# A hybrid decoder step: first rows scaled in pieces, and loads, stores and a product given other places

## Chip, cores and metric

The kernel runs on one core of one Trainium2 chip. The core has TensorE (PE in the profile) for matrix products and transposes, VectorE (DVE), ScalarE (ACT), GpSimd (POOL) and SyncE (SP), which issues most of the transfers between HBM and the on-chip memory; a transfer's work is done by 16 DMA engines. Each engine runs its own instructions in order, and semaphores make one wait for another. The metric is the device time of one execution in microseconds, as a median over runs.

## What is computed

One layer for a prompt of 2048 tokens behind 16 learned "meta" tokens, and one new token for each of 8 sequences that have a cache. The width is 1024. Eight attention heads of 64 use stick-breaking weights; four groups of 128 channels are averaged over trailing windows of 2, 4, 8 and 16 tokens. Cut to what matters:

```python
h = rmsnorm(xp, norm_mix_g)              # xp: 16 meta rows, then the prompt
q, k, v, u = project_mix(h, w_in)        # 1024 -> 4 x 512
z = q @ k^T * ATTN_SCALE + sb_bias       # per head, key before query
a = exp(log_sigmoid(z) + suffix sums of -softplus(z) over later keys)
o_pool = (window mean of u - u) @ pool_w * pool_scale    # per group
xp = xp + concat([a @ v, o_pool]) @ w_out
xp = xp + conv_ffn(rmsnorm(xp, norm_ffn_g))  # 1024 -> 2 x 2816, width-3 conv, silu gate, -> 1024
y = rmsnorm(xp, norm_final_g)
```

rmsnorm multiplies a row by 1/sqrt(mean of squares + 1e-6) and by a gain. The same runs for the eight new tokens against their cached keys and values.

## The kernel before

**Tiles and products.** The prompt is cut into four chunks of 512 tokens, the width into eight blocks of 128. The normalised input is kept transposed, a tile `hk` per block and chunk (128 features x 512 tokens), split into a high and a low part in a shorter float format (fp32r). A product in full precision is three matmuls (`mm3`, lines 164 to 168): high by high, high by low, low by high. Weights come as raw 128x1024 tiles `wr` and are split into `wh` (a cast on ACT, line 160) and `wl` (a subtraction on DVE, line 161).

**The start.** `prep_first` (line 236) loads the first four tiles of 128 rows, squares them on ACT with a sum per row (`squares`), makes 1/rms of all four at once (`rstd_from`, an integer guess and three Newton steps on DVE), scales each 128x1024 tile on DVE (`times_r`), and then calls `turned` for each block: four transposes on PE (line 222, tile `tpx`), the gain and the high part on ACT (line 225), the low part on DVE (226), and a spill of the pair to HBM, `hs_s`, by SP (228), from which later head pairs load it again. `prep_small` does the same for 24 rows (8 new tokens, 16 meta rows), kept as `hsml`.

**Projection and attention.** The work is cut by g into four groups: two heads and 128 pooled channels each. For each g, chunk and kind (q, k, v, u: `step(g, ch, ki)`) a projection of 24 matmuls writes a 128x512 tile `kf`, which goes to HBM as q_s, k_s or rows of the outputs. At the first chunk `load_w` brings the weights in pairs (q, k and then v, u), and `few_rows` runs the 24 rows through each pair, 32 small matmuls (line 302), a transpose (`tq`, line 307) and stores, of which the meta rows of keys, queries and values are needed by attention. While chunk ch is projected, `prep_squares` and `prep_piece` prepare chunk ch+1 (tiles `xp` of 256 columns). Behind (1, 3), `fold_pool` multiplies the group's pooling weights by four rows' blocks of w_out, so that pooling and output projection become one (`pkf`, `pkw`, lines 393 to 405).

Attention works on units of 128 queries by up to 512 keys, 45 for each pair of heads. `fetch` loads keys (line 469), values (487) and queries: a group of 256 queries of one head is a tile `qr`, whose 64 feature rows are loaded twice, into the upper and the lower half of the 128 partitions (lines 457 and 458), since the keys' high and low parts lie stacked there; the tile is split into `qh` and `ql`. The first group of a pair has the 16 meta queries alone. `chain` computes the scores `z` for each of the two heads (line 518), both sigmoids on ACT (`om`, `be`), the running product by a scan on DVE (529), and multiplies `be` by the shifted scan (534), for one head on GpSimd and for the other on DVE. `turn` transposes the result (`tt`, line 572) and `weigh` multiplies it by the values.

**What sets the order.** The list `fill` holds the projection steps and preparations in program order, with `with_params` (the conv parameters, turned by PE at lines 636 and 637, and sums of the pooling state) as second entry; the loop behind it calls as many fill steps ahead of each unit as its keys need. The compiler's scheduler then fixes each engine's instruction order by a timeline of its own. SP's queue holds the loads and stores of all these parts in one order.

Behind the attention come the output projection, the ConvFFN in two halves (tiles `psu` and `psd`, the larger part of the span) and the eight new tokens, which the change doesn't touch but for `rstd_from`.

Of the kernel before, what the change touches and what calls it, by code (L numbers as in the profile page):

```python
# [19 lines left out]
P = 128  # L20
# [41 lines left out]
def hymba_kernel(  # L62
# [74 lines left out]
    def rstd_from(pool, ss, n):  # L137

        w = ss.shape[1]
        ms = pool.tile([P, w], F32, name=f"ms{w}")  # L140
        nc.vector.tensor_scalar(out=ms[:n, :], in0=ss[:n, :], scalar1=1.0 / D, scalar2=EPS, op0=ALU.mult, op1=ALU.add)
# [3 lines left out]
        nc.vector.tensor_single_scalar(ti[:n, :], ms[:n, :].bitcast(I32), 1, op=ALU.logical_shift_right)  # L145
        nc.vector.tensor_scalar(out=ri[:n, :], in0=ti[:n, :], scalar1=-1.0, scalar2=float(0x5F3759DF),
                                op0=ALU.mult, op1=ALU.add)
        for _ in range(3):
            if w == 1:
                nc.vector.scalar_tensor_tensor(out=t[:n, :], in0=r[:n, :], scalar=r[:n, 0:1], in1=ms[:n, :],  # L150
                                               op0=ALU.mult, op1=ALU.mult)
            else:
                nc.vector.tensor_tensor(out=t[:n, :], in0=r[:n, :], in1=r[:n, :], op=ALU.mult)
                nc.vector.tensor_tensor(out=t[:n, :], in0=t[:n, :], in1=ms[:n, :], op=ALU.mult)
            nc.vector.tensor_scalar(out=t[:n, :], in0=t[:n, :], scalar1=-0.5, scalar2=1.5, op0=ALU.mult, op1=ALU.add)
            nc.vector.tensor_tensor(out=r[:n, :], in0=r[:n, :], in1=t[:n, :], op=ALU.mult)
# [44 lines left out]

    def load_x(i, tag, bufs):
# [15 lines left out]
    def turned(ch, c, part):  # L218
# [9 lines left out]
        nc.sync.dma_start(out=hs_s[ch][c], in_=f32(hk))  # L228
# [7 lines left out]
    def prep_first():  # L236
        ss = pb.tile([P, 4], F32, name="ss4")
        xts = [load_x(1 + a, "be", BEB) for a in range(4)]
        gains()
# [3 lines left out]
        for a in range(4):  # L243
            times_r(xts[a], r[:, a:a + 1])
        hks[0] = []
        for c in range(NK):
            turned(0, c, lambda a: xts[a][:, c * P:(c + 1) * P])
# [39 lines left out]
    def load_w(g, kind):  # L287
        ft = 4 * "qkvu".index(kind) + g
        wr = pa.tile([P, NK, P], F32, name="wr", bufs=2)
        nc.sync.dma_start(out=wr, in_=w_in[:, ft * P:(ft + 1) * P].rearrange("(c p) f -> p c f", p=P))  # L290
        wh = pa.tile([P, NK, P], F32R, name="wh", bufs=4)
        wl = pa.tile([P, NK, P], F32R, name="wl", bufs=4)
        split(wh, wl, wr)
        return wh, wl, wr

    def few_rows(g, pair, w):
# [3 lines left out]
        for c in range(NK):  # L300
            for j in range(2):
                nc.tensor.matmul(ps[32 * j:32 * j + 32, :], hsml[:, c, :], w[pair[j]][2][:, c, :],
# [45 lines left out]
    tails = {}  # L348
# [40 lines left out]

    def fold_pool(g):  # L390
# [862 lines left out]
```

## Time and profile before

| | us |
|---|---|
| three runs | 2767.65, 2768.55, 2773.09 |
| their median | 2768.55 |
| the profiled execution, its own time | 2771.54 |
| its span, first to last instruction | 2769.8 |
| ACT busy in the span | 1031.4 |

The profile is of one execution, 3.0 us above the median of the runs. Busy times don't count instructions that only issue transfers. Its 40 slices show where PE rests and at which granted clock (tenths; 9 is 90% or more):

```profile
PE   5899999999998999999999999999999999999998
PEclk9899999999999999999999999999999999999999
DMA  7653552454425433455556555646656574666551
```

A slice is 69 us: the first holds the start with half of PE's time unused, the second the first units of attention. The groups of costly instructions are nearly all the ConvFFN's products, at some 0.39 us each, which follow each other closely; the start of the program is therefore read from windows and waits, not from the groups.

### The profile page before, as it was taken

How to read it: one execution, taken by the hardware profiler on the slowest of the kernel's cores; microseconds unless marked ns; L12 is line 12 of the kernel's file. 1: busy time of each engine (PE TensorE's matmuls, PEld its weight loads, DVE VectorE, ACT ScalarE, POOL GpSimd, SP SyncE). 2: the span in 40 equal slices, each digit the busy share in tenths (PEclk: the TensorE clock that was granted, in tenths of full speed). 3: DMA queues.
4: the chain of work that ended last, by engine and by line, in shares of the span. 5: the costliest groups of instructions: out<-in, count | busy, mean ns of one | idle time of the engine just before them, and what ended most of it. 6: DMA issues, size and time to landing. Idle time of an engine off the chain costs nothing.

```text
span 2769.8 us, 39760 instructions
## 1 busy us (share of the span) xinstructions
PE 2662.7 (96%) x14759; PEld 2089.6 (75%) x14759; DVE 1805.2 (65%) x3037; ACT 1031.4 (37%) x1833; POOL 721.7 (26%) x736
## 2 busy tenths in 40 slices
PE   5899999999998999999999999999999999999998
PEld 4677777787786888778877777777776777777776
DVE  4588768857669588669977777777774541114434
ACT  4466656655557256423322222222222320012111
POOL 0012212211122011145554554445554200000000
PEclk9899999999999999999999999999999999999999
DMA  7653552454425433455556555646656574666551
GB/s 252 218 178 118 167 179 97 130 203 136 165 87 171 159 117 101 147 193 193 184 208 242 207 201 213 227 165 237 215 206 237 173 258 165 200 205 212 179 194 64
DMA packets 326375, 498.79 MB, mean 180 GB/s; under 512 B 25367, under 2 KB 238631, under 8 KB 309781
## 3 DMA queue, kind: packets, MB, share of 16 engines
q1 hardware_dynamic: 307749, 362.03, 39.8%
q0 software_dynamic: 18432, 134.23, 12.7%
q8 instruction: 116, 1.90, 0.3%
q14 instruction: 78, 0.64, 0.1%
HBM read 395.99 MB, written 100.59 MB: 179 GB/s over the span
## 4 chain that ended last, share of the span: by engine, by line
PE 79%; DVE 3%; issue 2%; DMA 2%; ACT 1%; POOL 0%; SPq 0%; DVEq 0%; ACTq 0%; POOLq 0%
PE psu L166 12%; PE psu L167 12%; PE psu L168 12%; PE psd L166 6%; PE psd L168 6%; PE psd L167 6%; PE po L615 4%; PE z L518 3%; PE tt L572 3%; PE dav L950 2%; PE psm L166 2%; PE psm L168 2%; PE psm L167 2%; PE pso L167 2%; PE pso L166 2%; PE pso L168 2%
## 5 line engine op out<-in xcount | busy, mean ns | idle before, releaser
L166 PE MATMUL psu<-h2c,uwh 128*128 128x512 f32 x1408 | 555.0, 394 | 4.0 <-ACT uwh L160 2.2
L168 PE MATMUL psu<-h2c,uwl 128*128 128x512 f32 x1408 | 550.7, 391 | 1.3 <-DVE uwl L161 1.3
L167 PE MATMUL psu<-h2c,uwh 128*128 128x512 f32 x1408 | 551.6, 392 | 0.0
L534 POOL TENSOR_TENSOR be<-be,om 128x512 f32<-128x512 f32 (+3 forms) x176 | 182.6, 1037 | 844.2 <-DVE om L529 302.0
L1048 DVE SCALAR_TENSOR_TENSOR cv<-psu,par,cv 128x511 f32<-128x511 f32 x352 | 261.2, 742 | 146.5 <-ACT cv L1045 142.9
L166 PEld LDWEIGHTS psu<-h2c,uwh 128*128 128x128 f32 x1408 | 265.2, 188 | 81.1 <-issue 10.9
L1059 POOL TENSOR_TENSOR cv<-cv,cv 128x512 f32<-128x512 f32 x88 | 224.7, 2554 | 388.6 <-DVE cv L1053 290.7
L168 PEld LDWEIGHTS psu<-h2c,uwl 128*128 128x128 f32 x1408 | 265.3, 188 | 63.7 <-issue 7.3
L167 PEld LDWEIGHTS psu<-h2c,uwh 128*128 128x128 f32 x1408 | 265.3, 188 | 62.1 <-issue 8.5
L529 DVE TENSOR_TENSOR_SCAN om<-om,zero 128x513 f32<-128x513 f32 (+1 forms) x224 | 274.0, 1227 | 46.2 <-ACT om L519 41.2
L519 ACT ACTIVATE om<-z,nbias 128x512 f32<-128x512 f32 (+5 forms) x360 | 213.3, 593 | 138.3 <-PE z L518 83.4
L1045 ACT ACTIVATE cv<-psu,par 128x512 f32<-128x512 f32 x176 | 136.4, 776 | 289.1 <-PE psu L168 289.1
L1220 DVE TENSOR_TENSOR xt<-psd,xt 128x512 f32<-128x512 f32 x64 | 44.0, 691 | 281.8 <-PE psd L168 281.7
L520 ACT ACTIVATE be<-z,bias 128x512 f32<-128x512 f32 (+5 forms) x360 | 211.4, 589 | 0.6 <-PE tt L572 0.6
L167 PE MATMUL psm<-hk,wh 128*128 128x512 f32 x512 | 206.6, 404 | 2.9 <-DVE hk L226 2.9
L166 PE MATMUL psm<-hk,wh 128*128 128x512 f32 x512 | 205.0, 406 | 1.9 <-ACT hk L225 1.3
L168 PE MATMUL psm<-hk,wl 128*128 128x512 f32 x512 | 204.2, 399 | 1.0 <-DVE wl L161 1.0
L161 DVE TENSOR_TENSOR uwl<-uwr,uwh 128x1024 fp32r<-128x1024 f32 x94 | 121.1, 1290 | 127.8 <-ACT uwh L160 127.8
L166 PE MATMUL psd<-wd,ah 128*128 128x512 f32 x512 | 200.3, 395 | 0.0
L167 PE MATMUL psd<-wd,ah 128*128 128x512 f32 x512 | 200.0, 392 | 0.0
L168 PE MATMUL psd<-wd,al 128*128 128x512 f32 x512 | 199.4, 390 | 0.0
L160 ACT CAST uwh<-uwr 128x1024 fp32r<-128x1024 f32 x94 | 98.8, 1054 | 246.4 <-PE psu L167 230.4
(245 smaller groups left out, 4773.8 us busy)
## 6 DMA issues: line engine op xcount, KB each, us to landing
hk<-hs_s SPq DMA_DIRECT2D x96, 512.0 KB
uwr<-in_w_up_dram SPq DMA_DIRECT2D x88, 512.0 KB
act_s<-sg SPq DMA_DIRECT2D x88, 256.0 KB
ar<-act_s SPq DMA_DIRECT2D x32, 704.0 KB
raw<-in_w_up_dram SPq DMA_DIRECT2D x40, 512.0 KB
xt<-in_x_prompt_dram SPq DMA_DIRECT2D x32, 512.0 KB
hs_s<-hk SPq DMA_DIRECT2D x32, 512.0 KB
uwr<-in_w_down_dram SPq DMA_DIRECT2D x22, 512.0 KB
```

The lines of the kernel that those rows point to most:

```text
L161: nc.vector.tensor_tensor(out=lo, in0=src, in1=f32(hi), op=ALU.subtract)
L166: nc.tensor.matmul(ps, ah, bh, start=i == 0, stop=False)
L167: nc.tensor.matmul(ps, ah, bl, start=False, stop=False)
L168: nc.tensor.matmul(ps, al, bh, start=False, stop=i == n - 1)
L519: nc.scalar.activation(out=om[:M, e, 0:n], in_=z[:M, :n], func=AF.Sigmoid, scale=-SCALE, bias=nbias[:M, h:h + 1])
L520: nc.scalar.activation(out=be[:M, e, 0:n], in_=z[:M, :n], func=AF.Sigmoid, scale=SCALE, bias=bias[:M, h:h + 1])
L529: nc.vector.tensor_tensor_scan(out=rv, data0=rv, data1=zero[:M, 0:1].broadcast_to([M, n + 1]), initial=st["prev"][:M, e, 0:1], op0=ALU.mul ...
L534: (nc.gpsimd if cnt["mul"] % 2 == 0 else nc.vector).tensor_tensor(out=be[:M, e, m0:n], in0=be[:M, e, m0:n], in1=om[:M, e, m0 + 1:n + 1], o ...
L615: mm = nc.tensor.matmul(o, v_, a_, start=start, stop=stop, skip_group_check=True).ins
L1045: nc.scalar.activation(out=t, in_=ps, func=AF.Identity, scale=cpar(2, fi), bias=cpar(3, fi))
L1048: nc.vector.scalar_tensor_tensor(out=t[:, o:], in0=ps[:, 0:CW - o], scalar=cpar(d, fi), in1=t[:, o:], op0=ALU.mult, op1=ALU.add)
L1059: nc.gpsimd.tensor_tensor(out=cv[1], in0=cv[0], in1=cv[1], op=ALU.mult)
```

## The change

1. `rstd_from` works on h = -0.5 (ss/D + eps), with another integer constant, and does the last two operations of a Newton step in one: three operations fewer in each chain (15 to 12 for four columns, 12 to 9 for one).
2. `prep_first` loads the gains first, and all four raw weight tiles of g = 0 right behind the rows (q, k as before, v, u as two halves each in the buffers of `vt`). The rows are scaled in pieces of 256 columns, two of four on ACT, and q's and k's weights are split between the pieces.
3. The spills of `hk` are issued by GpSimd.
4. `load_w` falls into `load_raw_w` and `split_w`; for g = 0 `few_rows` stands behind the projections of k and of v. `prep_small` and the pooling state's sums are fill steps behind the first step, the conv parameters are the thirteenth (`with_params` falls into `pool_sums` and `conv_params`, whose code is unchanged).
5. w_out's rows and the pooling weights for `fold_pool` are loaded by `fold_load`, two kinds earlier, into buffers of `wr` and `pl`.
6. A query tile is loaded by one DMA whose source repeats the 64 rows by an outermost dimension of size 2 and step 0.
7. GpSimd multiplies the first head of a unit, DVE the second.
8. The first unit's loads are called ahead of two further fill steps.

```diff
@@ -137,23 +137,22 @@
         w = ss.shape[1]
-        ms = pool.tile([P, w], F32, name=f"ms{w}")
-        nc.vector.tensor_scalar(out=ms[:n, :], in0=ss[:n, :], scalar1=1.0 / D, scalar2=EPS, op0=ALU.mult, op1=ALU.add)
+        h = pool.tile([P, w], F32, name=f"ms{w}")
+        nc.vector.tensor_scalar(out=h[:n, :], in0=ss[:n, :], scalar1=-0.5 / D, scalar2=-0.5 * EPS, op0=ALU.mult, op1=ALU.add)
         r = pool.tile([P, w], F32, name=f"rr{w}")
...
         ri, ti = r.bitcast(I32), t.bitcast(I32)
-        nc.vector.tensor_single_scalar(ti[:n, :], ms[:n, :].bitcast(I32), 1, op=ALU.logical_shift_right)
-        nc.vector.tensor_scalar(out=ri[:n, :], in0=ti[:n, :], scalar1=-1.0, scalar2=float(0x5F3759DF),
+        nc.vector.tensor_single_scalar(ti[:n, :], h[:n, :].bitcast(I32), 1, op=ALU.logical_shift_right)
+        nc.vector.tensor_scalar(out=ri[:n, :], in0=ti[:n, :], scalar1=-1.0, scalar2=float(0x9EF759DF),
                                 op0=ALU.mult, op1=ALU.add)
...
             if w == 1:
-                nc.vector.scalar_tensor_tensor(out=t[:n, :], in0=r[:n, :], scalar=r[:n, 0:1], in1=ms[:n, :],
+                nc.vector.scalar_tensor_tensor(out=t[:n, :], in0=r[:n, :], scalar=r[:n, 0:1], in1=h[:n, :],
                                                op0=ALU.mult, op1=ALU.mult)
...
                 nc.vector.tensor_tensor(out=t[:n, :], in0=r[:n, :], in1=r[:n, :], op=ALU.mult)
-                nc.vector.tensor_tensor(out=t[:n, :], in0=t[:n, :], in1=ms[:n, :], op=ALU.mult)
-            nc.vector.tensor_scalar(out=t[:n, :], in0=t[:n, :], scalar1=-0.5, scalar2=1.5, op0=ALU.mult, op1=ALU.add)
-            nc.vector.tensor_tensor(out=r[:n, :], in0=r[:n, :], in1=t[:n, :], op=ALU.mult)
+                nc.vector.tensor_tensor(out=t[:n, :], in0=t[:n, :], in1=h[:n, :], op=ALU.mult)
+            nc.vector.scalar_tensor_tensor(out=r[:n, :], in0=t[:n, :], scalar=1.5, in1=r[:n, :], op0=ALU.add, op1=ALU.mult)
         return r
@@ -225,7 +226,7 @@
                                        op0=ALU.mult, op1=ALU.subtract)
-        nc.sync.dma_start(out=hs_s[ch][c], in_=f32(hk))
+        nc.gpsimd.dma_start(out=hs_s[ch][c], in_=f32(hk))
         hks[ch].append(hk)
@@ -235,16 +236,25 @@
         ss = pb.tile([P, 4], F32, name="ss4")
+        gains()
         xts = [load_x(1 + a, "be", BEB) for a in range(4)]
-        gains()
+        raw_w.update({kind: load_raw_w(0, kind) for kind in "qkvu"})
         for a in range(4):
...
         r = rstd_from(pb, ss, P)
-        for a in range(4):
-            times_r(xts[a], r[:, a:a + 1])
         hks[0] = []
-        for c in range(NK):
-            turned(0, c, lambda a: xts[a][:, c * P:(c + 1) * P])
+        for q in range(4):
+            for a in range(4):
+                x_ = xts[a][:, 2 * P * q:2 * P * (q + 1)]
+                if a < 2:
+                    nc.scalar.mul(x_, x_, r[:, a:a + 1])
+                else:
+                    scaled = nc.vector.tensor_scalar(out=x_, in0=x_, scalar1=r[:, a:a + 1], scalar2=None, op0=ALU.mult).ins
+            for c in range(2):
+                turned(0, 2 * q + c, lambda a: xts[a][:, (2 * q + c) * P:(2 * q + c + 1) * P])
+            if q < 2:
+                with tc.issue_after(scaled):
+                    w["qk"[q]] = split_w(raw_w.pop("qk"[q]))
@@ -284,14 +294,26 @@
-    def load_w(g, kind):
+    def load_raw_w(g, kind):
         ft = 4 * "qkvu".index(kind) + g
+        wi = w_in[:, ft * P:(ft + 1) * P].rearrange("(c p) f -> p c f", p=P)
+        if g == 0 and kind in "vu":
+            wr = [pb.tile([P, 4, P], F32, name="vt", bufs=VTB) for _ in range(2)]
+            for i in range(2):
+                nc.sync.dma_start(out=wr[i], in_=wi[:, 4 * i:4 * i + 4, :])
+            return wr
         wr = pa.tile([P, NK, P], F32, name="wr", bufs=2)
-        nc.sync.dma_start(out=wr, in_=w_in[:, ft * P:(ft + 1) * P].rearrange("(c p) f -> p c f", p=P))
+        nc.sync.dma_start(out=wr, in_=wi)
+        return [wr[:, 0:4, :], wr[:, 4:NK, :]] if g == 0 else [wr]
+    def split_w(wr):
         wh = pa.tile([P, NK, P], F32R, name="wh", bufs=4)
         wl = pa.tile([P, NK, P], F32R, name="wl", bufs=4)
-        split(wh, wl, wr)
-        return wh, wl, wr
+        n = NK // len(wr)
+        for i, src in enumerate(wr):
+            split(wh[:, n * i:n * i + n, :], wl[:, n * i:n * i + n, :], src)
+        return wh, wl, lambda c: wr[c // n][:, c % n, :]
@@ -299,7 +321,7 @@
             for j in range(2):
-                nc.tensor.matmul(ps[32 * j:32 * j + 32, :], hsml[:, c, :], w[pair[j]][2][:, c, :],
+                nc.tensor.matmul(ps[32 * j:32 * j + 32, :], hsml[:, c, :], w[pair[j]][2](c),
                                  start=c == 0, stop=c == NK - 1, skip_group_check=True)
@@ -387,40 +409,47 @@
+    def fold_load(g):
+        wts[g] = pa.tile([P, NK, P], F32, name="wr", bufs=2).rearrange("p c n -> p (c n)")
+        nc.sync.dma_start(out=wts[g], in_=w_out[(4 + g) * P:(5 + g) * P, :])
+        pls[g] = pa.tile([P, P], F32, name="pl")
+        nc.sync.dma_start(out=pls[g], in_=pool_w[g])
     def fold_pool(g):
-        pl = pb.tile([P, P], F32, name="pl", tag="ot")
-        nc.sync.dma_start(out=pl, in_=pool_w[g])
+        pl = pls.pop(g)
         pk = tt_tile("pkf")
...
         for q in range(2):
-            wt = room("wt")[:, 0:CW]
-            nc.sync.dma_start(out=wt, in_=w_out[(4 + g) * P:(5 + g) * P, q * CW:(q + 1) * CW])
             pk = tt_tile("pkw").rearrange("p a b -> p (a b)")
-            nc.tensor.matmul(pk, pT, wt, start=True, stop=True)
+            nc.tensor.matmul(pk, pT, wts[g][:, q * CW:(q + 1) * CW], start=True, stop=True)
             wf = room("wf")[:, 0:CW]
...
-    w = {}
     def step(g, ch, ki):
...
             for kind in pair:
-                w[kind] = load_w(g, kind)
-            few_rows(g, pair, w)
+                if g or ki:
+                    w[kind] = split_w(raw_w.pop(kind) if g == 0 else load_raw_w(g, kind))
+            if g:
+                few_rows(g, pair, w)
         nxt = (ch + 1) % NCH
...
         project(g, ch, "qkvu"[ki], w["qkvu"[ki]], hk)
+        if (g, ch) == (0, 0) and ki in (1, 2):
+            few_rows(g, pair, w)
         if ahead:
             load_h(nxt, HKB - NK, NK)
+        if (ch, ki) == (1, 1):
+            fold_load(g)
         if (ch, ki) == (1, 3):
@@ -454,8 +483,7 @@
                 qr = pb.tile([P, CW], F32, name="qr", tag="raw", bufs=RWB)
-                nc.sync.dma_start(out=qr[0:DH, :gn], in_=q_s[hp][rows, g0:g0 + gn])
-                nc.sync.dma_start(out=qr[DH:P, :gn], in_=q_s[hp][rows, g0:g0 + gn])
+                nc.sync.dma_start(out=qr[:, :gn], in_=q_s[hp][rows, g0:g0 + gn].unsqueeze(0).broadcast_to([2, DH, gn]))
                 qh = pb.tile([P, QW], F32R, name=f"qh{e}", bufs=2)
@@ -531,7 +559,7 @@
                     cnt["mul"] += 1
-                    (nc.gpsimd if cnt["mul"] % 2 == 0 else nc.vector).tensor_tensor(
+                    (nc.gpsimd if cnt["mul"] % 2 else nc.vector).tensor_tensor(
                         out=be[:M, e, m0:n], in0=be[:M, e, m0:n], in1=om[:M, e, m0 + 1:n + 1], op=ALU.mult)
@@ -692,14 +723,15 @@
-    prep_small()
...
-            fill.append(with_params)
+            fill += [prep_small, pool_sums]
+        if len(fill) == 12:
+            fill.append(conv_params)
@@ -719,9 +751,11 @@
                    for u, n in enumerate(needs[:ui + 24]))
+        if ui == 0:
+            fill_to(first)
+            h[1](*un)
+            first += 2
         fill_to(max(want if ui else first, min(n_in, first + (n_in - first) * ui // END)))
-        if ui == 0:
-            h[1](*un)
         if ui + 1 < len(units):
```

How the scheduler places this is seen in three rows of instructions. The first is ACT's at the start of the program, of before and then of the change: `sq` are squares of rows (24x1024 the small ones), `wh` the high parts of weights, `vt` here v's and u's raw halves, `xt` a row piece.

```order
L209 ACTIVATE sq,ss_163<-xt 128x1024 x4
L209 ACTIVATE sq,ss<-xt 24x1024
L160 CAST wh<-wr 128x1024 x2
L209 ACTIVATE sq,ss_405<-xt 128x1024 x3
L225 ACTIVATE hk<-tpx,gcol 128x512
```

```order
L210 ACTIVATE sq,ss_163<-xt 128x1024 x4
L159 CAST wh<-wr 128x512 x4
L159 CAST wh<-vt 128x512
L250 ACTIVATE xt<-xt,rr_199 128x256 x8
L159 CAST wh<-vt 128x512 x3
L210 ACTIVATE sq,ss<-xt 24x1024
L226 ACTIVATE hk<-tpx,gcol 128x512 x2
```

All four weights' casts and eight pieces' scalings now stand ahead of the first `hk`; three of the next chunk's squares no longer do.

The second is PE's, where the projections of q and k end (before) and where those of v and u end (the change): `t` are the few rows, `pkp` the conv parameters, `pkg` the pooling state, `pk` transposes for the outputs.

```order
L168 MATMUL psm<-hk,wl 128x512
L302 MATMUL t_323<-wr,hsml 32x128 x16
L307 MATMUL tq<-ident,sm 128x64
L636 MATMUL pkp<-ident,ra 128x128
L166 MATMUL psm<-hk,wh 128x512
```

```order
L661 MATMUL pkg<-ident,sp 128x120
L375 MATMUL pk<-ident,kf 128x128 x4
L324 MATMUL t_451<-wr,hsml 32x128 x16
L329 MATMUL tq<-ident,sm 128x64
L375 MATMUL pk<-ident,kf 128x128 x4
L324 MATMUL t_528<-vt,hsml 32x128 x16
L329 MATMUL tq<-ident,sm 128x64
L223 MATMUL tpx<-ident,xp 128x128 x8
```

Both sets of few rows have moved behind all four projections of the first chunk, and the conv parameters' transposes out of this place.

The third is SP's queue at the first queries of 256 columns (before) and from the keys to them (the change), and PE's row at the scores that use the second pair of them (`qh_923` is of the first head, `qh_929` of the second).

```order
L457 DMA qr<-q_s_57 64x256
L458 DMA qr<-q_s_57 64x256
L457 DMA qr<-q_s_57 64x256
L458 DMA qr<-q_s_57 64x256
L457 DMA qr<-q_s_57 64x256
L458 DMA qr<-q_s_57 64x256
L259 DMA xp<-in_x_prompt_dram 128x4x256 x4
L357 DMA out_dram<-ko 128x4x128
L457 DMA qr<-q_s_57 64x256
L458 DMA qr<-q_s_57 64x256
```

```order
L497 DMA raw<-k_s_61 64x400
L509 DMA vtm<-out_dram 16x64 x2
L515 DMA vt<-out_dram 128x3x128
L486 DMA qr<-q_s_57 128x1x16 x2
L403 DMA cat_s<-dT 128x512
L486 DMA qr<-q_s_57 128x1x256 x2
L269 DMA xp<-in_x_prompt_dram 128x4x256 x3
L486 DMA qr<-q_s_57 128x1x256 x2
```

```order
L223 MATMUL tpx<-ident,xp 128x128 x10
L165 MATMUL psm<-hk,wh 128x512 x2
L546 MATMUL z<-kst_569,qh_923 128x400
L546 MATMUL z<-kst_574,qh_929 128x400
L223 MATMUL tpx<-ident,xp 128x128 x4
```

In SP's queue one load stands for two, the values' loads stand ahead of the first queries, and three `xp` pieces stand ahead of both tiles of the second pair, where before four stood ahead of its second tile alone; in PE's row the scores of that pair now stand behind transposes and two products of the next chunk.

More of the change, by code (lines that the diff above doesn't have):

```diff
@@ L200, in hymba_kernel @@
     gcol = pa.tile([P, NK], F32, name="gcol")
+    w, raw_w = {}, {}
     def load_x(i, tag, bufs):
@@ L346, in window_sums @@
         return src
-    tails = {}
+    tails, wts, pls = {}, {}, {}
     def put_tok(dst, g, ch, src):
@@ L626, in weigh, with pool_sums, conv_params @@
                 end()
-    def with_params():
-        ra, rb, sp = room("ra")[:, 0:P], room("rb")[:NPR - P, 0:P], room("sp")[:15 * NS, 0:512]
+    def pool_sums():
+        sp = room("sp")[:15 * NS, 0:512]
+        nc.sync.dma_start(out=sp, in_=state_pool.rearrange("b j f -> (b j) f"))
+        for g, w in enumerate(WIN):
+            tg = tt_tile("pkg").rearrange("p a b -> p (a b)")[:, 0:15 * NS]
+            nc.tensor.transpose(tg, sp[:, g * P:(g + 1) * P], ident[:15 * NS, :15 * NS])
+            nc.vector.tensor_reduce(out=spool[:, g, :],
+                                    in_=tg.rearrange("p (b j) -> p b j", j=15)[:, :, 16 - w:],
+                                    axis=AX.X, op=ALU.add)
+    def conv_params():
+        ra, rb = room("ra")[:, 0:P], room("rb")[:NPR - P, 0:P]
         cw = conv_w.rearrange("i (f p) -> (i f) p", p=P)
@@ L638, in with_params @@
         nc.vector.tensor_copy(par, tp)
-        nc.sync.dma_start(out=sp, in_=state_pool.rearrange("b j f -> (b j) f"))
-        for g, w in enumerate(WIN):
-            tg = tt_tile("pkg").rearrange("p a b -> p (a b)")[:, 0:15 * NS]
-            nc.tensor.transpose(tg, sp[:, g * P:(g + 1) * P], ident[:15 * NS, :15 * NS])
-            nc.vector.tensor_reduce(out=spool[:, g, :],
-                                    in_=tg.rearrange("p (b j) -> p b j", j=15)[:, :, 16 - w:],
-                                    axis=AX.X, op=ALU.add)
     wo, out_pool = [], {}
```

## The prediction

> **What bounds the kernel now.** I read the page first, then windows over the whole span, then ten-microsecond windows of the start, and at last waits and timeline where these show holes. The page gives the span and each engine's busy time:
>
> ```profile
> span 2769.8 us, 39760 instructions
> PE 2662.7 (96%) x14759; PEld 2089.6 (75%) x14759; DVE 1805.2 (65%) x3037; ACT 1031.4 (37%) x1833; POOL 721.7 (26%) x736
> ```
>
> PE (TensorE) sets the time. The change leaves its products as they are, so only two things can move: the 107.1 us in which PE has nothing to run, and the time lost to a slow clock. The next windows (length, then busy time and count of PE, PEld, DVE, ACT and POOL, then granted clock, DMA share, GB/s) put both at the start: 87.1 us of the idle time lie before 1150 us, 4.6 in the turn to the second half and 15.4 behind it.
>
> ```profile
> 0.00:1150.00 1150.00, 1062.93 (x7176) 849.70 (x7176) 837.16 (x1497) 649.37 (x1341) 203.40 (x420) 0.98 0.46 153
> 1150.00:1168.00 18.00, 13.39 (x69) 10.31 (x67) 13.40 (x30) 7.29 (x13) 0.00 (x0) 0.91 0.87 252
> 1168.00:2769.80 1601.80, 1586.39 (x7519) 1229.62 (x7517) 954.62 (x1510) 374.79 (x479) 518.29 (x316) 1.00 0.58 199
> ```
>
> ```profile
> 40.00:50.00 10.00, 4.70 (x15) 3.64 (x16) 4.35 (x15) 4.97 (x7) 0.21 (x2) 0.66 0.73 214
> ...
> 70.00:80.00 10.00, 6.43 (x26) 5.59 (x27) 9.48 (x26) 5.78 (x11) 2.73 (x5) 0.53 0.48 153
> ...
> 120.00:130.00 10.00, 6.03 (x19) 3.97 (x18) 1.71 (x3) 2.54 (x4) 0.00 (x0) 0.67 0.49 162
> ...
> 140.00:200.00 60.00, 53.71 (x365) 42.68 (x364) 51.83 (x97) 38.62 (x82) 11.71 (x24) 0.97 0.48 161
> ```
>
> The ten-microsecond windows show the holes. Each costs twice: PE idles, and the granted clock is down to 0.66, 0.53 and 0.67 beside it. PE's waits name what ends the holes (total, times, longest), and two places in its timeline show the slow clock: products follow each other by 0.43 us at 47.25 and by 0.23 us at 49.03.
>
> ```profile
> PE pkp L636 <- DMA ra<-in_conv_w_dram: 6.1, 1, 6.1
> PE z L518 <- ACT qh L160: 6.0, 1, 6.0
> PE z L518 <- DVE ql L161: 2.4, 1, 2.4
> PE pkw L402 <- DMA wt<-in_w_out_dram: 4.0, 1, 4.0
> PE tt L572 <- POOL om L513: 10.3, 6, 2.6
> ```
>
> ```profile
> 47.25 0.63 PE L167 MATMUL psm<-hk,wh 128*128 128x512 f32 x1
> 47.68 0.63 PE L168 MATMUL psm<-hk,wl 128*128 128x512 f32 x1
> ...
> 49.03 0.39 PE L166 MATMUL psm<-hk,wh 128*128 128x512 f32 x1
> 49.26 0.40 PE L167 MATMUL psm<-hk,wh 128*128 128x512 f32 x1
> ```
>
> **The first product: -0.3 us.** The timeline (start, length, engine, line) before the first product:
>
> ```profile
> 10.03 1.06 ACT L209 ACTIVATE sq<-xt 128x1024 bf16<-128x1024 f32 x1 [0.81 <-DMA xt<-in_x_prompt_dram]
> ...
> 10.99 0.18 ACT L209 ACTIVATION_READ_ACCUMULATOR sq<-xt 128x1 f32 x1
> ...
> 11.21 0.17 DVE L141 TENSOR_SCALAR ms<-ss 128x4 f32<-128x4 f32 x1 [0.68 <-ACT sq L209]
> ...
> 13.83 1.04 ACT L160 CAST wh<-wr 128x1024 fp32r<-128x1024 f32 x1 [0.68 <-DMA wr<-in_w_in_dram]
> ...
> 17.03 2.74 DVE L232 TENSOR_SCALAR xt<-xt,rr 128x1024 f32<-128x1024 f32 x4
> ...
> 21.32 0.67 ACT L225 ACTIVATE hk<-tpx,gcol 128x512 fp32r<-128x512 f32 x1
> ...
> 22.05 0.73 PE L166 MATMUL psm<-hk,wh 128*128 128x512 f32 x2 [1.31 <-ACT hk L225]
> ```
>
> A 128x256 pass on ACT, the size of a piece, stands in the groups of instructions (count, busy us, mean ns):
>
> ```profile
> L160 ACT CAST qh<-qr 128x256 fp32r<-128x256 f32 x64 | 26.0, 410 | 34.9 <-PE z L518 21.3 <-DMA qr<-q_s 13.3 <-DVE om L527 0.3
> ```
>
> The chain from sums to scaling runs 11.21 to 17.03; three fewer operations and no second chain between them end it near 14. But ACT's order decides what follows: k's second half is cast at 13.83 + 0.6, then one half of v (0.6), eight scalings (0.41 each, overlapping by the 0.1 that the entries at 10.03 and 10.99 show: 2.5 us), three more halves (0.6 each), the small rows' squares (1.06 and 0.18), and only then hk. The raw halves land 0.85 us apart if 512 KB takes 1.7, as it did for k. That ends v's first half at 15.3, the scalings at 17.8, the halves at 19.6 and the squares near 20.9, so hk at 21 and the first product at 21.7 instead of 22.05. If ACT didn't run the halves first it could be 17.5 (-4.5); if a half lands late it is later (+2). I take the order's figure.
>
> **The conv parameters: -8.0 us.** PE's 6.1 us wait for ra, 0.3 us around it and the slow clock behind it go: seven products at 0.43 instead of 0.23 are 1.4, in all about 1.6 with the transpose. Behind the first two products now stand v's, whose halves were cast before hk. The transpose comes back under unit work, long after ra is there. Uncovered again, it would cost the 6.1. The few rows keep their 32 products and so don't count.
>
> **The first queries: +5 us.** Timeline rows on today's order, from the few rows of q and k to the first queries, and then the end of 14 products of chunk 1:
>
> ```profile
> 36.58 1.94 PE L302 MATMUL t<-wr,hsml 128*32 128x128 f32 x32
> ...
> 46.02 0.35 SPq L386 DMA_DIRECT2D k_s<-kf  x1
> ...
> 50.08 1.18 SPq L469 DMA_DIRECT2D raw<-k_s  x2
> ...
> 54.30 0.60 SPq L458 DMA_DIRECT2D qr<-q_s  x1
> ...
> 56.27 0.20 ACT L160 CAST qh<-qr 128x16 fp32r<-128x16 f32 x1 [2.05 <-DMA qr<-q_s]
> ...
> 82.34 0.62 PE L166 MATMUL psm<-hk,wh 128*128 128x512 f32 x2
> ```
>
> One transfer of few rows in the timeline, a window in which only it is in flight, and two lines of the page on the queue (packets, MB, share of 16 engines) and on the query loads (count, KB):
>
> ```profile
> 11.56 0.66 SPq L1072 DMA_DIRECT2D out_dram<-in_state_pool_dram  x1
> ```
>
> ```profile
> 16.20:17.20 1.00, 0.00 (x0) 0.00 (x0) 1.00 (x11) 0.84 (x2) 0.00 (x0) 1.00 0.54 229
> ```
>
> ```profile
> q1 hardware_dynamic: 307749, 362.03, 39.8%
> ...
> qr<-q_s SPq DMA_DIRECT2D x128, 64.0 KB
> ```
>
> Today a query load lands 1.4 us behind the end of its issue (54.90 to 56.27). The merged load has an outermost source dimension of 2. The trace shows a transfer with an outermost dimension of 8, the state copy of L1072: alone in flight at 16.20, it keeps 0.54 of the 16 engines busy, which is eight or nine. I read this as a sharing-out by that dimension, so the merged load would run on two engines: 64 KB on each of them for a 128 KB load. The queue's 362.03 MB in 39.8% of 16 engines' span are 20.5 KB/us for one, so a load takes 3.1 us and a pair 6.2 (the least estimate is today's 1.4, if the outermost dimension doesn't decide). The Trainium skill says the same in "DMA: Bandwidth & Descriptors", under "Rules for kernel authors": a leading zero-stride broadcast of c < 16 copies confines the DMA to at most c engines. By the Trainium skill's 27 GiB/s for an engine, an estimate, a load would take 2.3 us and the sum would come out some 3 us lower; the 0.54 agrees with the rule, and no trace here shows an outermost 2.
>
> When are they issued? The few rows now stand behind v's and u's 48 products (0.23 each, 10.9 us) and 1.4 us of transposes: 22 + 14.5 + 10.9 + 1.4, about 48.5 for 36.58. Before, k's rows were loaded 13.5 us behind the few rows, some 5 of them due to k's own store, issued at 46.02, that now lies far ahead: about 57, and the queries, behind two more loads that wait for stores, near 60. PE has run out of products at about 60. The first 256-wide pair lands at 65 and 68; three xp pieces of 512 KB (32 KB on each engine, 1.6 us) stand ahead of the next pair, which lands near 75.5 and 78.5, so the last z of the first unit is at 79.5. By then PE has done 20 transposes and 14 products of chunk 1 more than the kernel before had at its z, a point which that reaches at 82.8 (the last of these rows). With two small products left over, I get 2.6 us ahead there, of 8.3 that were won: 5.7 given back, rounded to 5 since PE's clock suffers no more than before. With loads on 16 engines it would be 4.5 won instead.
>
> **The fold: -6.9 us.** w_out's rows are now issued far ahead, so the 4.0 us wait at L402 goes, and 2.9 of slow clock with it: nearly half of the 6.03 us that PE ran in 120:130, much of it at half speed (0.67 granted on the mean). What is late next is the queries' and xp's landing, as in the last part; on wide loads another 3 us would go.
>
> **Delays at 140 to 200: +3.** PE idles 6.3 us there. The pairs of the next units and the xp pieces behind them come up to 6.2 us later on two engines. Nothing to all of it is uncovered; +3 is the middle, near the longest wait for a query so far (4.9, below).
>
> **The rest: -0.4.** Two groups on POOL (count, busy, mean ns), one line of ACT's waits, and the last chain:
>
> ```profile
> L534 POOL TENSOR_TENSOR be<-be,om 128x512 f32<-128x512 f32 x72 | 92.2, 1280 | 385.6 <-DVE om L529 162.8 <-ACT sq L134 48.2 <-ACT at L565 30.4
> L867 POOL DMA_INDIRECT kvd<-in_cache_k_dram,idx x64 | 81.5, 1274 | 71.1 <-DVE zdec L882 27.7 <-PE dav L950 16.2 <-DVE carry L1055 9.6
> ```
>
> ```profile
> ACT qh L160 <- DMA qr<-q_s: 17.1, 11, 4.9
> ```
>
> ```profile
> 2764.50 0.15 DVE L155 TENSOR_SCALAR rt<-rt 128x1 f32<-128x1 f32 x1
> ```
>
> GpSimd's product (1.28 us) starts a scan earlier, on the first head: of the 10.3 us that PE waits for POOL's side I take 3 (bounds 0 and 10). Later query loads: ACT waits 17.1 us for 11 of 72 today, most of it off PE's path; I add 3 for one uncovered pair (bounds 0 and 30 pairs, rival 2). The last chain loses three operations of 0.15 at the end: -0.4. The 32 spills go to GpSimd's queue: by the nearest issue there, 1.27 us, 41 us beside 203 busy of 1150, hidden; if a weighing stood behind one, it would cost 1.3. SP issues 72 fewer loads at 0.6, which nothing on PE's path waits for.
>
> **Sum:** -0.3 - 8.0 + 5 - 6.9 + 3 - 0.4 = -7.6. The profiled execution took 2771.54 (its span is 2769.8), so 2763.9 on it; the runs have a median of 2768.55, 3.0 lower, so I predict 2761.0.
>
> **Rivals.** (1) *Wide query loads.* Sharing-out isn't by that dimension: -0.3 - 8.0 - 4.5 - 10 + 0 - 3.4 = -26, 2742.4. For it: the destination has 128 partitions. Against it: the 0.54. (2) *The narrow loads become the bound: slower.* Two engines carry 64 x 64 KB more each, 4.1 MB or 200 us of the first 1150, beside the 46% that all have. If ten of the 30 later pairs come uncovered, at 2.8 us (the 3.1 of its second load less the slack), 28 stand in place of 3: +17.4, 2786. It decides from three pairs beyond the forecast's one (7.6 / 2.8). For it: loads stand in one queue with all stores. Against it: in 72 loads ACT waits 17.1 us today, so most land with time to spare. (3) *The shorter chain does carry*, and products start at 17.5: -4 more, 2757; against it stands ACT's order. That the headline change alone does nothing is the forecast itself.
>
> **How the numbers follow.** Forecast 0.50, its own range 2752 to 2770; rival 1 0.25; rival 2 0.17; rival 3 0.08. The range 2742 to 2782 takes in rival 1 and the near part of rival 2. A measurement of this kernel can tell about 0.2%, 5.5 us, from no change. The forecast is split 0.27 faster, 0.21 same, 0.02 slower; rivals 1 and 3 are faster but for 0.01, and rival 2 is slower but for 0.01: faster 0.59, same 0.23, slower 0.18.
>
> **What would show it.** First product at 21 to 22; no wait for ra or w_out, and clock 1.00 until 60; a 3 us landing of query loads and a wait at the first units' z; the idle time before 1150 near 82. A landing under 2 us means rival 1; waits of z for queries all along the 1150 us mean rival 2; a first hk before 19 means rival 3. Wrong altogether: new waits on GpSimd's spills.

## The result and the profile after

The changed kernel takes 2801.47 us in the median of three runs (2797.56 to 2801.55), against 2768.55 before: a ratio of 1.011, with a 95% interval of 1.0087 to 1.0133. It is slower. The profiled execution took 2801.55 us, 30.0 more than the one of before.

The page of the changed kernel gives span and busy times; below them stand windows that end, as before, at the turn to the second half (length, busy time and count by engine, granted clock, DMA share, GB/s):

```profile
span 2799.8 us, 39715 instructions
PE 2678.8 (96%) x14759; PEld 2096.9 (75%) x14759; DVE 1797.8 (64%) x2928; ACT 1034.8 (37%) x1845; POOL 754.0 (27%) x768
```

```profile
0.00:1180.00 1180.00, 1079.66 (x7172) 857.76 (x7174) 838.41 (x1445) 652.37 (x1353) 236.12 (x452) 0.97 0.45 150
...
1198.00:2799.80 1601.80, 1585.45 (x7521) 1228.73 (x7519) 946.49 (x1456) 375.21 (x479) 517.88 (x316) 1.00 0.58 199
```

The 30 us come in two parts. PE is idle for 121.0 us instead of 107.1, so 13.9 more; and the same 14,759 matmuls keep it busy 16.1 us longer (2678.8 against 2662.7), which is mostly slow clock behind the idle time: the mean granted clock is 0.983 instead of 0.988, and over the span that is 14 us. The whole of it lies ahead of the second half, whose last 1601.8 us have the same products and the same idle time within a microsecond. Ahead of the turn PE idles 100.3 us, where the forecast had 82 and the kernel before 87.1.

Windows of the start of the changed kernel, in the stretches in which the prediction read holes:

```profile
40.00:50.00 10.00, 10.00 (x60) 8.26 (x60) 2.01 (x13) 4.04 (x7) 0.21 (x2) 1.00 0.49 179
...
60.00:70.00 10.00, 0.81 (x5) 0.32 (x4) 2.73 (x8) 1.89 (x8) 0.48 (x3) 0.78 0.63 179
70.00:80.00 10.00, 6.72 (x22) 4.74 (x22) 6.62 (x20) 4.91 (x12) 1.20 (x3) 0.54 0.48 147
80.00:90.00 10.00, 7.21 (x22) 5.80 (x23) 5.05 (x11) 2.78 (x5) 2.30 (x5) 0.66 0.55 221
```

The hole at 40 to 50 is gone; in its place PE has 0.81 us of work between 60 and 70 and runs on a slow clock until 90. The waits of PE over the whole span (total, times, longest) say for what:

```profile
PE z L546 <- ACT be L548: 16.0, 21, 2.2
PE z L546 <- ACT qh L159: 15.0, 6, 5.2
PE tpx L223 <- ACT xt L250: 11.7, 1, 11.7
PE tpx L223 <- DVE xp L233: 8.2, 3, 5.8
...
PE tt L600 <- DVE be L562: 3.1, 5, 1.3
PE tt L600 <- POOL om L541: 2.2, 6, 0.7
...
PE tt L600 <- POOL be L562: 2.1, 4, 0.8
```

The conv parameters and w_out no longer appear; scores that wait for queries (15.0 us against 8.4 for high and low part before) and for sigmoids (16.0 against 8.9) and pieces of the next rows (8.2 against 6.0) have grown. All six waits for queries lie between 60 and 84 us. ACT's waits and the timeline of SP and ACT at the first queries show the loads behind it:

```profile
ACT qh L159 <- DMA qr<-q_s: 41.7, 21, 3.5
```

```profile
64.56 1.55 SPq L486 DMA_DIRECT2D qr<-q_s  x2
66.16 4.25 SPq L269 DMA_DIRECT2D xp<-in_x_prompt_dram  x3
70.51 4.05 SPq L486 DMA_DIRECT2D qr<-q_s  x2
74.67 2.71 SPq L669 DMA_DIRECT2D ra<-in_conv_w_dram  x1
```

```profile
70.38 0.40 ACT L159 CAST qh<-qr 128x256 fp32r<-128x256 f32 x1 [3.49 <-DMA qr<-q_s]
73.15 0.40 ACT L159 CAST qh<-qr 128x256 fp32r<-128x256 f32 x1 [2.37 <-DMA qr<-q_s]
...
80.05 0.41 ACT L159 CAST qh<-qr 128x256 fp32r<-128x256 f32 x1 [1.36 <-DMA qr<-q_s]
82.78 0.40 ACT L159 CAST qh<-qr 128x256 fp32r<-128x256 f32 x1 [2.33 <-DMA qr<-q_s]
```

Two things are to be seen. Query tiles of a pair land 2.77 and 2.73 us apart. And SP itself is held up: it takes 4.25 us to issue three loads and 2.71 to issue one that usually takes some 0.35. Over the first 1150 us, 47 of SP's issues take more than 1 us, 90 us together, against 23 with 34 us before (counted, as all such counts below, from the traces' issue records).

Where the loss gathers is seen from fixed points of the program, each a group of SP's transfers with its first and last start. The first pair of rows is of the changed kernel, the second of the kernel before:

```profile
L282 SPq DMA_DIRECT2D hk<-hs_s x96: 314/395/2570, 205.6 to 807.2; - x96
...
L723 SPq DMA_DIRECT2D h_s<-xn x16: 320/332/333, 927.4 to 1193.6; - x16
```

```profile
L272 SPq DMA_DIRECT2D hk<-hs_s x96: 319/376/1424, 197.1 to 790.9; - x96
...
L692 SPq DMA_DIRECT2D h_s<-xn x16: 319/332/338, 902.0 to 1163.9; - x16
```

These are the reloads of hk and the stores of the output projection's rows. The change is 8.5 us late at the first point, 16.3 at the second, 25.4 at the third and 29.7 at the fourth: not one stall, but a delay that grows through all of attention.

### The profile page after: what moved, and what is told of

Its sections match the earlier page's. It is cut to its first block, busy times and chain, and to the rows that moved or that the text cites. A ratio compares the mean times of both kernels' runs of the same rounds, so it can differ in the third digit from the quotient of the medians.

```text
span 2799.8 us, 39715 instructions
## 1 busy us (share of the span) xinstructions
PE 2678.8 (96%) x14759; PEld 2096.9 (75%) x14759; DVE 1797.8 (64%) x2928; ACT 1034.8 (37%) x1845; POOL 754.0 (27%) x768
## 3 DMA queue, kind: packets, MB, share of 16 engines
q1 hardware_dynamic: 300437, 345.24, 37.9%
## 4 chain that ended last, share of the span: by engine, by line
PE 84%; DMA 7%; DVE 5%; issue 2%; ACT 2%; SPq 0%; POOL 0%; DVEq 0%; ACTq 0%; POOLq 0%
PE psu L165 12%; PE psu L166 11%; PE psu L167 11%; PE psd L165 6%; PE psd L167 6%; PE psd L166 6%; PE po L643 4%; PE psm L165 4%; PE psm L166 4%; PE psm L167 4%; PE z L546 3%; PE tt L600 3%; PE dav L984 2%; PE pso L166 2%; PE pso L165 2%
## 5 line engine op out<-in xcount | busy, mean ns | idle before, releaser
L562 POOL TENSOR_TENSOR be<-be,om 128x512 f32<-128x512 f32 (+3 forms) x176 | 193.4, 1099 | 643.5 <-DVE om L557 280.0
L1082 DVE SCALAR_TENSOR_TENSOR cv<-psu,par,cv 128x511 f32<-128x511 f32 (+1 forms) x352 | 261.1, 742 | 144.0 <-ACT cv L1079 142.5
L557 DVE TENSOR_TENSOR_SCAN om<-om,zero 128x513 f32<-128x513 f32 (+1 forms) x224 | 281.3, 1267 | 48.0 <-ACT om L547 46.8
```

Source lines behind the costliest of these rows:

```text
L557: nc.vector.tensor_tensor_scan(out=rv, data0=rv, data1=zero[:M, 0:1].broadcast_to([M, n + 1]), initial=st["prev"][:M, e, 0:1], op0=ALU.mul ...
L562: (nc.gpsimd if cnt["mul"] % 2 else nc.vector).tensor_tensor(out=be[:M, e, m0:n], in0=be[:M, e, m0:n], in1=om[:M, e, m0 + 1:n + 1], op=ALU ...
L1082: nc.vector.scalar_tensor_tensor(out=t[:, o:], in0=ps[:, 0:CW - o], scalar=cpar(d, fi), in1=t[:, o:], op0=ALU.mult, op1=ALU.add)
```

## Experiments

**Theory 1**: the merged query load, with its outermost dimension of 2, runs on two engines, lands late and costs the time (the forecast's own mechanism and that of rival 2, with another size). **Theory 2**: the other moves and the new order cost it. Four runs, the first two meant to leave every engine's order as it was (in e1, PE's is the changed kernel's for the first 315 us; in e2 all of it is that of before).

### The merged load made wide, and the loads of before made narrow

Of each load the source alone is shown.

```diff
  # e1, in the changed kernel
- q_s[hp][rows, g0:g0 + gn].unsqueeze(0).broadcast_to([2, DH, gn])
+ q_s[hp][:, g0:g0 + gn]
  # e2, in the kernel before, both loads
- q_s[hp][rows, g0:g0 + gn]
+ q_s[hp][rows, g0:g0 + gn].rearrange("(a b) n -> a b n", a=2)
  # e3: the changed kernel with the two loads of before
  # e4: the kernel before with the merged load
```

> The changed kernel, but each merged query load takes the 128 rows of both heads once (outermost dimension 128) instead of one head's 64 rows twice; same bytes, same count of loads, so the scores are of wrong queries, and every engine's order stays as it is for the first 760 or so rows of PE. Theory 1 (the merged loads land late because an outermost dimension of 2 puts them on two engines): loads land within 2 us, ACT's waits for queries fall from 41.7 us below 20, PE's 13 us loss at 60 to 100 us goes, and the time is 2745 to 2765 us. Theory 2 (the loss comes from the other moves: GpSimd's first head and spills, later few rows, another order): 2790 to 2802 us.

> The kernel before, with nothing changed but the shape in which each of its two 64-row query loads is written: 2 x 32 rows instead of 64. All engines keep their order, row for row. Theory 1: each load lands on two engines, a pair of tiles takes some 5.5 us as in the changed kernel, and the time is 2785 to 2805 us. Theory 2: 2766 to 2772 us, as before.

> The changed kernel with the two 64-row query loads of before in place of the merged load (the one part undone; the scheduler then orders all engines anew). Theory 1: 2742 to 2765 us, ACT's waits for queries below 20 us. Theory 2: 2790 to 2805 us.

> The kernel before with the merged query load alone (the scheduler orders anew). Theory 1: 2785 to 2810 us, with single loads 2.7 us apart in landing. Theory 2: 2763 to 2772 us, since SP saves 72 issues.

| run | us, median | ratio to before, 95% interval |
|---|---|---|
| e1, plain rows | 2759.63 | 0.9955 (0.9939 to 0.9972) |
| e2, 2 x 32 rows | 2771.59 | 0.9999 (0.999 to 1.0009) |
| e3, two loads | 2764.07 | 0.9973 (0.9961 to 0.9984) |
| e4, merge alone | 2828.92 | 1.0206 (1.0189 to 1.0223) |

Theory 1 holds in e1, e3 and e4: with 128 plain rows in one load the changed kernel is 0.45% faster than before instead of 1.1% slower, a difference of 42 us in the medians (the kernel before lay at 2768.6 us in the first round and at 2770.8 to 2771.9 in later ones, so up to 3 us of such differences can be drift); the merge alone makes the kernel before 2.1% slower, more than expected. In e1 ACT hardly waits for queries, and a pair lands 1.0 us apart:

```profile
ACT qh L159 <- DMA qr<-q_s: 8.7, 6, 3.7
```

```profile
68.60 0.40 ACT L159 CAST qh<-qr 128x256 fp32r<-128x256 f32 x1
69.60 0.41 ACT L159 CAST qh<-qr 128x256 fp32r<-128x256 f32 x1 [0.59 <-DMA qr<-q_s]
```

The hole behind 60 us was expected to go in e1, but only part of it does: between 60 and 100 PE idles 9.7 us, against 15.5 in the change and 9.5 before. The fixed points of e1 are:

```profile
L282 SPq DMA_DIRECT2D hk<-hs_s x96: 319/376/1408, 187.0 to 772.9; - x96
...
L723 SPq DMA_DIRECT2D h_s<-xn x16: 320/332/333, 890.3 to 1153.7; - x16
```

Against these the changed kernel is 18.6 us late at the first point, 34.3 at the second, 37.1 at the third and 39.9 at the fourth.

e2 is a miss as an experiment: ACT's wait for queries is 17.2 us, as it was with 17.1, so its loads landed as before and nothing was narrowed. The page agrees: its count of packets is that of before, as the next part reads it. A shape of 2 x 32 rows with equal steps isn't the same as a repetition. It says nothing of either theory.

### How many engines: a series

Of a load of 128 rows, 128/n are read and repeated n times; all engines' orders are those of the changed kernel, row for row.

```diff
- q_s[hp][rows, g0:g0 + gn].unsqueeze(0).broadcast_to([2, DH, gn])
+ q_s[hp][0:P // n, g0:g0 + gn].unsqueeze(0).broadcast_to([n, P // n, gn])   # e5: n = 4, e6: 8, e7: 16
```

> The changed kernel, its merged query load written as 32 rows repeated 4 times instead of 64 repeated twice (wrong queries, same bytes and rows landed, all engines' orders unchanged row for row). Theory A (the outermost dimension sets the number of engines): a load is spread over four, some 1.4 us instead of 2.7; more than half of the 42 us are won back: 2765 to 2782 us. Theory B (the repetition itself is slow: the same HBM rows read again, or a step of 0): about 2800 us.

> The same with 16 rows repeated 8 times. Theory A: eight engines, 2759 to 2768 us. Theory B: about 2800 us.

> The same with 8 rows repeated 16 times. Theory A: sixteen engines, as with 128 plain rows: 2757 to 2763 us. Theory B: about 2800 us.

| outermost dimension | us, median | ratio, 95% interval | ACT's waits for queries, us | packets of SP's queue |
|---|---|---|---|---|
| 2 (the change) | 2801.47 | 1.011 (1.0087 to 1.0133) | 41.7 | 300437 |
| 4 | 2772.16 | 1.0009 (1.0 to 1.0019) | 26.8 | 300581 |
| 8 | 2768.47 | 0.9987 (0.9977 to 0.9997) | 19.6 | 300869 |
| 16 | 2765.89 | 0.9983 (0.9974 to 0.9993) | 19.2 | 301445 |

The last column is from the pages' rows on the queues, here of the change and of e1:

```profile
q1 hardware_dynamic: 300437, 345.24, 37.9%
```

```profile
q1 hardware_dynamic: 301445, 345.24, 38.7%
```

The bytes are the same, and yet there are 14, 12 and 8 packets fewer for each of the 72 loads at 2, 4 and 8 than at 16 (72 x 14 = 1008). In the packet records the missing ones are all of 4 bytes. That is what one closing packet on each engine of a load would give, with 2, 4, 8 and 16 engines; so the number of engines shows in a count, and not only in the time. The kernel before and e2 both have 307749 packets: e2's loads ran on as many engines as those of before.

The repetition isn't what is slow: 16 repetitions cost nothing like 2. The time falls with the outermost dimension, as theory A has it, and steeply: 29 of 36 us are won by going from 2 to 4. With 4, SP's long issues are down to 19 with 32 us as well (22 with 31 at 16). e6 and e7 lie a little above what was expected, 6 us behind e1's plain rows at 16. The e1 kernel's order differs from the others' in its later part, so that last piece isn't explained. Nor are single landings as regular as the sums: with 4, the first 256-wide pair lands 3.97 us apart and the second 1.32.

### The same loads narrowed in the kernel before, with its order kept

```diff
- q_s[hp][rows, g0:g0 + gn]                      # both 64-row loads
+ q_s[hp][e * DH:e * DH + DH // n, g0:g0 + gn].unsqueeze(0).broadcast_to([n, DH // n, gn])   # e13: n = 2, e14: 16
```

> The kernel before, each of its two 64-row query loads written as 32 rows repeated twice (wrong queries, same bytes; every engine's order as before, row for row, which the 2 x 32 form of run e2 did not put to the test since its loads landed as before). If the outermost dimension of 2 is the whole cause, the narrow loads cost about the 42 us that separate the changed kernel from its plain-row form: 2795 to 2815 us. If a good part of the changed kernel's loss is due to how its new order meets late queries: 2775 to 2790 us.

> Control: the same loads as 4 rows repeated 16 times. Sixteen engines: 2767 to 2774 us, as before. If the repetition costs by itself: above 2776 us.

e13 took 2820.56 us, ratio 1.017 (1.0151 to 1.0189); its control e14 2772.46, ratio 1.0001 (0.9992 to 1.0011). So 48 us by an outermost dimension of 2 and nothing else, in a program that has none of the change. That is a little more than expected and settles the cause. The packets agree: e14 has the 307749 of before, e13 14 fewer for each of its 144 loads (305733). In e13 the timeline of SP shows the queue held up at the first queries as in the changed kernel, and in e14 not:

```profile
61.76 5.35 SPq L259 DMA_DIRECT2D xp<-in_x_prompt_dram  x4
```

```profile
59.85 2.77 SPq L259 DMA_DIRECT2D xp<-in_x_prompt_dram  x4
```

Over the first 1150 us, 48 of SP's issues take more than 1 us in e13, 84 us together, against 16 with 24 us in e14. The queue is held up all along, by loads that differ in their outermost dimension alone.

### Late landing or a jammed queue?

```diff
- nc.sync.dma_start(out=qr[:, :gn], in_=q_s[hp][rows, g0:g0 + gn].unsqueeze(0).broadcast_to([2, DH, gn]))
+ nc.gpsimd.dma_start(out=qr[:, :gn], in_=q_s[hp][rows, g0:g0 + gn].unsqueeze(0).broadcast_to([2, DH, gn]))
```

> The changed kernel with its merged query loads issued by GpSimd instead of SP, still 64 rows repeated twice. Theory L (late landing of the queries is what costs): a load on two engines lands as late, 2790 to 2810 us. Theory S (SP's queue is jammed: the loads hold back what SP issues behind them, 47 issues of over 1 us with 90 us in all against 16 with 24 us in the plain-row run): SP's queue is free again and the time is 2765 to 2785 us.

It took 2783.71 us, ratio 1.0051 (1.0036 to 1.0066): 18 us less than the change, 20 more than e3. ACT still waits 34.9 us for queries, but only 7 of SP's issues in the first 1150 us are over 1 us (12 us). That is in theory S's range, at its upper end. So both seem to count; taken as it stands, the run gives them about equal parts. But the edit moves more than the queue: the 72 issues take 59 us of GpSimd's own time (0.82 each), the pages' counts give a load some 245 packets in GpSimd's queue and 130 in SP's, GpSimd's queue may place each narrow load on other engines than SP's does, which would spread them too, and the order of all engines is a new one. The split stays open.

### Which of the other parts pay

```diff
  # e8: the changed kernel, each head's 64 query rows stored twice, loaded as 128 plain rows
  # (the meta rows' stores and the tile of twice the rows are left out here)
+ for j in range(4):
+     nc.sync.dma_start(out=q_s[g][DH * j:DH * j + DH, t0:t0 + CW], in_=kf[j // 2 * DH:j // 2 * DH + DH, :])
+ nc.sync.dma_start(out=qr[:, :gn], in_=q_s[hp][e * P:(e + 1) * P, g0:g0 + gn])
  # e10: e3 with the weighing's heads as before
- (nc.gpsimd if cnt["mul"] % 2 else nc.vector)
+ (nc.gpsimd if cnt["mul"] % 2 == 0 else nc.vector)
...
  # e11: e3 with the spills as before
- nc.gpsimd.dma_start(out=hs_s[ch][c], in_=f32(hk))
+ nc.sync.dma_start(out=hs_s[ch][c], in_=f32(hk))
  # e12: e3 with the loads of four units first
- h[1](*un)
+ for h_, un_ in units[:4]:
+     h_[1](*un_)
```

> The changed kernel with each head's queries stored twice in HBM (four stores of 64 rows for one of 128), so that one load of 128 plain rows brings a query tile: the right result with one load and all engines. Theory A: near the plain-row run, 2757 to 2768 us, and not slower than the two-load version's 2764 by over 4. Theory B gives the same; the rival here is that 48 more stores of SP cost as much as 72 loads saved: 2764 to 2775 us.

> The two-load version of the changed kernel (ratio 0.9973) with the weighing's heads as before: DVE the first, GpSimd the second. The forecast had 3 us for GpSimd first: 2765 to 2769, ratio 0.998 to 0.9995. Rival: the turn over is worth nothing here, ratio 0.9965 to 0.998, or less if GpSimd first harms.

> The two-load version with the spills of hk issued by SP again. The forecast: hidden on GpSimd either way, ratio 0.9965 to 0.998. Rival: the spills stand in front of GpSimd's weighings and cost up to 10 us of what the wide form should win; ratio 0.993 to 0.996.

> The two-load version with the loads of the first four units called ahead of the next chunk's last pieces, so that the second pair of query tiles stands ahead of the xp pieces in SP's queue. If that order is what gives back the 8 us won by the conv parameters (PE waits 9.3 us for queries and 5.8 for xp in the two-load version), 4 to 6 us are won: ratio 0.995 to 0.9963. Rival: xp lands as much later as the queries land earlier and nothing changes, ratio 0.9965 to 0.998.

| run | us, median | ratio, 95% interval |
|---|---|---|
| e3, two loads (from above) | 2764.07 | 0.9973 (0.9961 to 0.9984) |
| e8, stored twice | 2767.97 | 0.9987 (0.9977 to 0.9996) |
| e10, DVE first | 2767.24 | 0.9988 (0.9979 to 0.9997) |
| e11, spills by SP | 2756.55 | 0.9946 (0.9932 to 0.9959) |
| e12, queries ahead of xp | 2769.1 | 0.9992 (0.9983 to 1.0001) |

e8 is no faster than two loads: 72 loads saved and 60 stores added. e10 loses 3 us, as forecast, but its interval overlaps e3's. e12 was to win 4 to 6 us and lost 5, though the intervals touch: PE's wait for queries fell from 9.3 to 8.1 us, the one for xp rose from 5.8 to 6.9.

e11 is the fastest version with the right queries: 14 us under the median of before in the same rounds (2770.8), 0.54% by the ratio. It wins 7.5 us over e3, but its trace doesn't say that the spills were what cost: PE's waits for GpSimd's side are 5.0 us there and 7.2 in e3. The row that falls most is another, PE's wait for xp pieces (1.1 us against 5.8), while its waits for queries and for sigmoids are each 2 us longer. The last row of the output projection is stored at 1150.0 instead of 1152.6, and by the first cast of h2c from tp3c in the ConvFFN (1245.9 against 1252.3) another 3.8 us are won, in a stage without spills. That part can't be the spills' own time; the new order of the whole program is the likely cause, which is not shown. e8, e10, e11 and e12 each reorder all engines, so differences of 3 to 8 us among them aren't pinned on their edits.

## Why the prediction was wrong, step by step

- **The first product (-0.3):** right in kind; it starts at 21.09 instead of 22.05, and rival 3, with a first hk before 19, is out. The timeline of the changed kernel shows the small rows' squares as the last thing ahead of hk, as worked out:

```profile
14.57 3.30 ACT L250 ACTIVATE xt<-xt,rr 128x256 f32<-128x256 f32 x8
...
17.77 1.64 ACT L159 CAST wh<-vt 128x512 fp32r<-128x512 f32 x3
...
19.32 1.05 ACT L210 ACTIVATE sq<-xt 24x1024 bf16<-24x1024 f32 x1
20.37 1.23 ACT L226 ACTIVATE hk<-tpx,gcol 128x512 fp32r<-128x512 f32 x2
...
21.09 1.22 PE L165 MATMUL psm<-hk,wh 128*128 128x512 f32 x2 [3.14 <-ACT hk L226]
```

  The scalings run from 14.57, on a chain that is short enough, and hk comes six microseconds later: the headline of the change is worth 1 us here.
- **The conv parameters (-8.0):** right in kind and nearly in size. PE is busy for 40.12 of the first 60 us instead of 34.26, and the granted clock is 1.00 there. With an estimated 1.6 us that the clock of 0.66 cost between 40 and 50 before (4.70 us busy there), this is 7.5 us won, of the 8.3 of this term and the one above.
- **The first queries (+5):** the mechanism was right, the size not. The last tile was to land at 78.5 and its z to run at 79.5; the cast stands at 82.78 and the z at 83.24. A narrow load took 2.75 us, not 3.1. The Trainium skill's figure, 27 GiB/s for an engine in "DMA: Bandwidth & Descriptors" under "Specifications", gave an estimate of 2.3; the measurement lies between. What the step left out is SP: xp's three pieces were issued in 4.25 us instead of some 1.3 (0.434 is the median issue of one before). That makes about +9 for this step instead of +5, by the same count of work done. Nor does PE's clock suffer "no more than before": it is 0.66 from 80 to 90, where the kernel before has 1.00.
- **The fold (-6.9):** the wait for w_out is gone, 0.6 us are left at that place. It was given back nearby, which the term didn't have: some 17 us behind the fold PE waits 5.8 us for an xp piece (4.8 in e3, with its wide loads, 19 us behind it). The longest such wait before is 2.0 us.
  The row of e3:

```profile
130.90 1.94 PE L223 MATMUL tpx<-ident,xp 128*128 128x128 f32 x8 [4.81 <-DVE xp L233]
```

- **Later queries (+3 at 140 to 200, +3 for the rest):** this is the step that failed. It counted one uncovered pair behind 200 us, because most loads have slack today, and costed SP's queue at nothing. Runs e1 and e13 put the narrow load at 42 and 48 us, where the forecast and rival 1 lie 18.6 apart. The fixed points say where: up to the first reload of hk, near 200 us, narrow loads cost 18.6 us (the change against e1), which is near the 15.6 that the forecast has there over rival 1; behind it they cost 21.3, where the term had 3.

  The way was another too. In the changed kernel PE's scores wait for no query behind 84 us. But ACT runs its instructions in order, and between 200 and 1200 us it waits for query loads 18.1 us against 4.7 in e1, and for keys, whose loads stand in the same queue, 59.8 against 36.8; so sigmoids come late, and PE waits for them 14.6 us against 9.8. In e13 against e14 the same three pairs are 13.4 and 5.0, 61.0 and 54.9, 16.1 and 9.0. These rows don't make up the whole 21 us. A wait also costs a second time in clock: of the 30 us over the kernel before, some 14 are that.

  Rival 2, with 2786 and a chance of 0.17, had the loads and the direction right and priced ten uncovered pairs at 28 us. But its mark, scores that wait for queries all along, did not come: it too left out that everything behind a narrow load in SP's queue comes later.
- **GpSimd first (-3):** about right; e10 gives 3 us, with overlapping intervals. PE's waits for GpSimd's side fell from 10.3 to 4.3 us (the rows om and be), and that for DVE's product rose from 0.7 to 3.1.
- **Spills hidden:** not shown. An issue takes GpSimd 0.56 us (18 us for all 32) and not 1.27. e11 without them is 7.5 us faster, about half of it in a stage that has no spills.
- **Rival 1 (-26 with wide loads):** e1 gives 11, e3 7. Up to the first reload of hk it had -22.8, and e1 is 10.1 us early there (187.0 against 197.1). Two of the parts that lack are seen in the traces. One is the xp piece behind the fold, above. The other is the first queries: the few rows that they need moved behind four projections, their loads are issued at 64 us instead of 51, and PE waits for them 9.3 us in e3, wide as they are. A step moved off one hole had been the start of a chain into the next.

The rule on a repetition that stands outermost, cited in the prediction from the Trainium skill's "DMA: Bandwidth & Descriptors" ("Rules for kernel authors"), is borne out by e5 to e7 and e13: 2, 4 and 8 repetitions leave 14, 12 and 8 packets fewer a load than 16, and the time falls from 2 to 16. The row of 0.54 on which the prediction rests held the packets of two copies, since those of L1071 end at 16.59, but both have an outermost dimension of 8, so the reading stands.

## What to carry to other kernels

One transfer in place of two saves an issue of half a microsecond, and can cost far more if its outermost dimension is small: look at that dimension before counting issues, and keep 16 or more rows outermost. The packet count of the queue on the page tells whether a load ran on fewer engines. When a transfer gets slower, price all that stands behind it in its queue, and all that stands behind the instruction that waits for it, not only who reads it. An edit that lets a scheduler reorder a program moves the time by some microseconds by itself; a form of the same shape and count (a repetition of other rows) tests a cause with the order kept.

## What the runs showed that was not expected

SP's issues are held up when narrow loads stand in its queue: behind the first 20 us there are single issues of up to 4.1 us in the changed kernel and 6.0 in e13, where 0.4 is the median and e1 has none over 2.9. This was gone with four engines (long issues of 32 us in all, as with sixteen, against 90). The cost of a narrow load isn't in proportion to its length: halving it from two engines to four won 29 us, the next halving 4 and the next 3, the last within the noise. A dimension of 2 with a step that continues the rows (e2) is not narrow; one with a step of 0 is.
